# Layer 1's feed forward by seven products of halves, in program order

## The chip, the core and the metric

The kernel runs on one core of one Trainium2 chip. The metric is the time of one execution in microseconds of device time. A core has five engines that run side by side, each taking its own instructions in order: PE (TensorE, matrix products), DVE (VectorE), ACT (ScalarE), POOL (GpSimd) and SP, which issues the DMA transfers here.

## The reference

Two layers of a transformer block over 512 latent and 256 context tokens of width 1024. Cut to what the change touches:

```python
def swiglu(h, w1, w3, w2):
    return (jax.nn.silu(h @ w1) * (h @ w3)) @ w2
...
    x = x + gt1 * merge_branches(...)
    x = x + gt2 * swiglu(modulate(rms_norm(x, norm2[l]), sh2, sc2), w_ff1[l], w_ff3[l], w_ff2[l])
```

Layer 0 does this for all 768 tokens, layer 1 (the last) for the 512 latent tokens only. The hidden width is 2816, which is 22 blocks of 128.

## The kernel before

Everything is fp32, and each product is made from split operands: a tile x is cut into a rounded part `hi` and the rest `lo = x - hi`, and a product of 128x128 weights with activations is three matmuls (w_hi a_hi, w_hi a_lo, w_lo a_hi). `split` (L293) issues the cast of `hi` on ACT (L294) and the subtraction of `lo` on DVE or POOL (L295). Activations lie with channels on the partitions and tokens along the free axis, so a matmul's width is the number of tokens it takes.

Weights come in pieces of 128x512 floats (256 KB) into a ring of five `ws` tiles, and their `hi` and `lo` go into rings of four (`wh`, `wl`).

**Layer 0's feed forward** takes blocks in pairs. `ff_pair` makes the two blocks of a pair for the two halves of the tokens (384 each) by seven products instead of eight, in the manner of Strassen and Winograd: once for w1 with silu, once for w3 with the multiplication. Each of the two calls `pair_product` (L423), whose seven products need four sums of weight pieces (s1, s2, s4, s3, on DVE, L341), seven casts on ACT, six `lo` subtractions on DVE and one on POOL. In `pair_product`, a PSUM bank A takes products 1, 3, 5 and 7, a bank B products 2 and 4, a bank C product 6; between them ACT copies what A or B holds at that point (L444, L447, L449, L453), and the next product adds on to the same bank. The activations' sums, which the pairs share, are made once by `pair_forms` from the norm's output. `flow` (L317) prepares each piece three products ahead. This part stands under `tc.manual_schedule()`, so the engines execute it in the order in which it is written; elsewhere a scheduler sets the order. The first pair (blocks 0 and 1) is done by `first_pair` with plain products of halves, during which `pair_forms` runs. The output products (w2) take the results four blocks at a time, in the parts (0,4), (4,8) and so on.

**Layer 1's feed forward** is written differently: `plain` makes each block with 24 matmuls for w1 and 24 for w3, 512 tokens wide (block 0 in two halves of 256 while the norm still runs), then `keep_u` splits the result, and `ff2_j` makes the output products of the blocks 0 to 7, 8 to 14 and 15 to 21. The scheduler sets the order of it all. Before it, `lagged(wo_j, ...)` makes the attention output products and the norm, half by half.

Of the kernel before, what the change touches and what calls it, by code (L numbers as in the profile page):

```python
# [16 lines left out]
P = 128  # L17
# [13 lines left out]
CS = (SEQ, NT)  # L31
HT = NT // 2
NG = 2
WM0 = 4
# [6 lines left out]
def dit_block(ctx: ExitStack, tc: tile.TileContext, xT, ctxn, conds, vecs, ident_in, rope_c, rope_s,  # L41
# [69 lines left out]

    arena, homes = {}, ["AB"]

    def new_arena(*which):
        for i in which:
            tag = homes[0][i // 8]
            arena[i] = big.tile([P, 4 * HT], F32R, tag=tag, name=tag, bufs=8)

    def unit(i, n=HT):
        return arena[i // 4][:, i % 4 * HT:i % 4 * HT + n]  # L120

    def pair_at(i, n=HT):
        step = 1 if n <= HT else 2
        return unit(i, n), unit(i + step, n)
# [157 lines left out]
    def cut_piece(st, n, kinds="hl"):  # L282
        lo_rot[0] += 1
        eng = lo_engs[0][lo_rot[0] % len(lo_engs[0])]
        if kinds == "bb":
            t = big.tile([P, 4 * HT], F32R, tag=homes[0][1], name="wb", bufs=8)
# [105 lines left out]
    def half_of(k, t):  # L392
        return pair_at(8 * (k % 4) + 4 * t + 2 * (k // 4))

    def sum_of(i, kk):
        return pair_at(32 + 8 * kk + 4 * (i % 2) + 2 * (i // 2))

    def split_two(t, u, eng):

        d = arena[u // 4].rearrange("p (v h n) -> p h v n", h=2, n=HT)  # L400
        split(t, d[:, 0], d[:, 1], eng)

    def pair_forms(Y, kk):

        y = Y[kk].rearrange("p (b n) -> p b n", n=HT)
        new_arena(8 + 2 * kk, 9 + 2 * kk)

        def two_forms():
            t = big.tile([P, 2 * HT], F32, tag="tf", name="tf", bufs=2)
            return t.rearrange("p (b n) -> p b n", n=HT)  # L410
        ta = two_forms()
        nc.vector.tensor_tensor(ta, y[:, 0:4:3], y[:, 1:2].to_broadcast([P, 2, HT]), op=ALU.subtract)
        tb = two_forms()
        nc.vector.tensor_tensor(tb[:, 0], y[:, 3], ta[:, 0], op=ALU.add)
        split_two(ta, 32 + 8 * kk, nc.vector)
        nc.vector.tensor_tensor(tb[:, 1], y[:, 2], tb[:, 0], op=ALU.subtract)
        split_two(tb, 36 + 8 * kk, nc.vector)

    def four(name):

        return [area(name) for i in range(4)]

    def pair_product(take, tmp, ev11, ev12, ev21, ev22, extra):  # L423
# [14 lines left out]
        def bank():  # L438
            return next_bank()[:, :HT]

# [82 lines left out]
    def norm_half(X, G, S, t, Y):  # L523

        a, b = t * HT, (t + 1) * HT
        RB = norm_stats(X, a, b)
        yield
        if t == 0:
            for kk in range(4):
                Y[kk] = big.tile([P, 4 * HT], F32, tag="Y", name="Y", bufs=PAIRS["Y"])  # L530
        for kk in range(4):
            y4 = Y[kk].rearrange("p (b n) -> p b n", n=HT)
# [62 lines left out]
    for l in range(2):  # L595
# [641 lines left out]
        gate_src = Z[7][0]  # L1237
        h2 = new_h(W) if last else new_halves()
        Y2 = {}
# [15 lines left out]

        if last:
            lagged(wo_j, segs, halves, lambda p: norm(Xn, G2[l], MOD[l][:, 3], *p, h2))
        else:
            lagged(wo_j, segs, [(0, HT), (HT, NT)], lambda p: norm_half(Xn, G2[l], MOD[l][:, 3], p[0] // HT, Y2))
        X = Xn  # L1260


        def plain(f0, f1, U):
            for n in range(f0, f1):
                first = n == 0
                sg = halves if first else segs
                su = area("su", W)

                def ev1(D, a, b):
                    nc.scalar.activation(su[:, a:b], D, AF.Silu)  # L1270

                def ev3(D, a, b):
                    nc.vector.tensor_tensor(su[:, a:b], su[:, a:b], D, op=ALU.mult)
# [18 lines left out]
        def first_pair(U):  # L1292

            su = [area("su") for _ in range(2)]
            ks = (0, 4, 1, 5, 2, 6, 3, 7)
            ww = {}

            def go(n, i, t):
                o = su[n][:, t * HT:(t + 1) * HT]
                turn[0] += 1  # L1300
                D = wide[turn[0] % 2][:, turn[0] // 2 % 2 * 512:][:, :HT]
                mm([D], [ww[n, i][k] for k in ks], [half_of(k, t) for k in ks], [(0, HT)])
                if i == 0:
# [14 lines left out]
        def ff_pair(m, U, take):  # L1318
            sa, sb = area("su"), area("su")
            a1, a2, b1, b2 = sa[:, :HT], sa[:, HT:], sb[:, :HT], sb[:, HT:]  # L1320

# [33 lines left out]

        def ff_layer_0(parts):

            items = []
            for f0, f1 in parts:
                items += [(True, w_13[l, i, 2 * m:2 * m + 2]) for m in range(f0 // 2, f1 // 2) if m for i in range(2)]  # L1360
                if f1 < NFF:
                    items += [(False, w_2[l, j][:, f0:f1, :].rearrange("p k n -> p (k n)")) for j in range(KD)]
            U = []
            first_pair(U)
            with tc.manual_schedule():
                for _ in range(3):
                    load_1()
                take = flow(items)
                for pi, (f0, f1) in enumerate(parts):
                    if pi:  # L1370
                        U, spot[0] = [], 0
                    for m in range(f0 // 2, f1 // 2):
                        if m:
                            ff_pair(m, U, take)
                    if f1 == NFF:
# [3 lines left out]
                    w, D = {}, {}  # L1379

                    def some(j, ks):
                        if j not in w:
                            wh, wl = take(j == 1)
                            w[j] = [(wh[:, i:i + P], wl[:, i:i + P]) for i in range(0, 512, P)]
                            D[j] = [next_bank() for _ in segs]
                        for k in ks:
                            mm(D[j], w[j][k:k + 1], U, segs, k=k)

                    for j in range(KD):
                        if j == 0:  # L1390
                            some(0, (0, 1))
                            some(1, (0, 1))
                            some(0, (2, 3))
                        else:
                            some(j, range(4) if j > 1 else (2, 3))
                        if j >= 2 or pi > 1:
                            sums_layer_1()
                        for d, (a, b) in zip(D[j], segs):
                            c = int(a >= SEQ)
                            nc.vector.scalar_tensor_tensor(X[j][:, a:b], d[:, :b - a], MOD[l][:, 5, j, c:c + 1],  # L1400
                                                           X[j][:, a:b], op0=ALU.mult, op1=ALU.add)

        parts = [(0, 8), (8, 15), (15, 22)] if last else [(0, 4), (4, 8), (8, 12), (12, 16), (16, 22)]
        if not last:
            U = ff_layer_0(parts)
            new_wide()
            parts = parts[-1:]
        for pi, (f0, f1) in enumerate(parts):
            if last:
                U = []  # L1410
                plain(f0, f1, U)
            if f1 == NFF and not last:
                homes[0] = "BA"
                hnext = new_h()
            def ff2_j(j, sg):
                w = load_w(w_2[l, j][:, f0:f1, :], f1 - f0)

# [4 lines left out]
                gemm(w, U, sg, ev)  # L1422
                if f1 == NFF:
                    a, b = sg[0][0], sg[-1][1]
                    if last:
                        nc.sync.dma_start(out[j], X[j][:, :SEQ])
                    else:
                        nc.sync.dma_start(xspill[j][:, a:b], X[j][:, a:b])

            if f1 == NFF and not last:  # L1430
                lagged(ff2_j, segs, halves, lambda p: norm(X, G1[1], MOD[1][:, 0], *p, hnext), KD)
            else:
                for j in range(KD):
                    ff2_j(j, segs)

# [64 lines left out]
```

## Time and profile before

| | us |
|---|---|
| median of 3 runs | 1927.59 (1927.42 to 1928.4) |
| the profiled execution's own time | 1930.93 |
| its span, from the first to the last instruction | 1929.1 |
| PE busy in that span | 1866.0 (97%) |
| DVE, ACT and POOL busy | 1143.4, 823.4, 702.4 |
| from layer 1's first feed forward matmul to the end of the span | 1561.57 to 1929.1 |

Matmuls overlap, so a row's duration of one matmul is longer than the distance to the next; the distance is read from the chain of waits or the timeline, as the length of a piece over its count. In a timeline row stand the start, the duration, the engine, the line, the operation, the tiles, and in brackets the idle time before it and what ended that.

### The profile page before, as it was taken

The numbers are of one execution on the slowest core, as the hardware profiler recorded it, in microseconds if no ns is written. First come the engines' busy times: TensorE is split into PE (matmuls) and PEld (weight loads), VectorE is DVE, ScalarE is ACT, GpSimd is POOL, SyncE is SP. The second block draws the span as 40 slices with busy tenths as digits, with TensorE's granted clock in tenths as the row PEclk, the third lists the DMA queues.
The fourth block names the chain that finished last, engine by engine and source line by source line (L and its number), as shares of the span: only waits on it lengthen the run. The fifth ranks groups of instructions, "written<-read, shape, count | busy, mean of one in ns | idle before, by whom it ended". The sixth has DMA issues, their size and how long they took to land.

```text
span 1929.1 us, 27661 instructions
## 1 busy us (share of the span) xinstructions
PE 1866.0 (97%) x10146; PEld 1647.7 (85%) x10146; DVE 1143.4 (59%) x1866; ACT 823.4 (43%) x1544; POOL 702.4 (36%) x572
## 2 busy tenths in 40 slices
PE   5998999999999899999999999999999999999999
PEld 4778989888889899998989988878788888888887
DVE  7678886586456978876767675267633461222222
ACT  3546866422224534342525455456533353233232
POOL 4543543442223322122222457653332343333231
PEclk9999999999999999999999999999999999999999
DMA  8653210343354143435342263321033443333333
GB/s 301 219 204 102 70 50 29 120 159 121 105 212 136 46 133 111 152 108 164 116 159 98 80 210 102 105 64 33 19 108 99 142 124 96 98 99 89 103 95 96
DMA packets 109449, 225.58 MB, mean 117 GB/s; under 512 B 12288, under 2 KB 21248, under 8 KB 109184
## 3 DMA queue, kind: packets, MB, share of 16 engines
q1 hardware_dynamic: 108208, 221.96, 35.8%
q10 hardware_dynamic: 1104, 1.84, 0.3%
q8 instruction: 80, 1.31, 0.3%
q14 instruction: 57, 0.47, 0.1%
HBM read 215.89 MB, written 5.24 MB: 115 GB/s over the span
## 4 chain that ended last, share of the span: by engine, by line
PE 55%; DVE 3%; ACT 1%; issue 1%; POOL 1%; DMA 0%; ACTq 0%; DVEq 0%; POOLq 0%
PE pD L304 17%; PE wide L304 16%; PE pE L435 12%; PE pE L304 5%; PE pF L304 2%; PE pO L1157 1%; PE pPT L1150 1%; PE wide L1124 1%; DVE nm L1128 1%; POOL u L295 0%; DVE ny L495 0%; DVE pt L1154 0%; ACT work L1131 0%; DVE B L500 0%; DVE nacc L471 0%
## 5 line engine op out<-in xcount | busy, mean ns | idle before, releaser
L295 POOL TENSOR_TENSOR wl<-ws,wh 128x512 fp32r<-128x512 f32 (+2 forms) x274 | 364.4, 1333 | 745.5 <-ACT wh L294 704.1
L294 ACT CAST wh<-ws 128x512 fp32r<-128x512 f32 (+2 forms) x534 | 322.2, 608 | 675.8 <-PE pD L304 219.1
L295 DVE TENSOR_TENSOR wl<-ws,wh 128x512 fp32r<-128x512 f32 x260 | 199.8, 770 | 311.9 <-ACT wh L294 309.5
L304 PE MATMUL wide<-B,wh 128*128 128x512 f32 (+1 forms) x816 | 230.6, 372 | 4.5 <-DVE B L500 1.9
L304 PE MATMUL pD<-B,wh 128*128 128x512 f32 (+1 forms) x720 | 218.4, 384 | 0.1
L304 PE MATMUL wide<-A,wh 128*128 128x512 f32 (+2 forms) x608 | 162.2, 360 | 13.4 <-POOL A L295 6.6
L304 PEld LDWEIGHTS wide<-B,wh 128*128 128x128 f32 x816 | 144.9, 189 | 33.1 <-DVE B L500 2.5
L435 PE MATMUL pE<-B,wh 128*128 128x384 f32 x640 | 162.6, 334 | 1.1 <-ACT work L444 1.0
L304 PEld LDWEIGHTS pD<-B,wh 128*128 128x128 f32 x720 | 134.1, 189 | 26.4 <-POOL B L295 0.3
L304 PE MATMUL wide<-B,wl 128*128 128x512 f32 (+1 forms) x408 | 143.8, 373 | 0.1
L304 PE MATMUL pD<-B,wl 128*128 128x512 f32 (+1 forms) x360 | 138.0, 384 | 0.0
L181 DVE SCALAR_TENSOR_TENSOR work<-work,fixed 128x1024 f32<-128x1024 f32 x80 | 112.7, 1408 | 37.2 <-DMA work<-in_w_modT 35.4
L304 PEld LDWEIGHTS wide<-A,wh 128*128 128x128 f32 x608 | 105.6, 191 | 33.4 <-POOL A L295 8.7
L304 PE MATMUL pD<-A,wh 128*128 128x512 f32 (+1 forms) x544 | 130.6, 349 | 0.1
L435 PE MATMUL pE<-A,wh 128*128 128x384 f32 x480 | 121.8, 334 | 0.0
L435 PEld LDWEIGHTS pE<-B,wh 128*128 128x128 f32 x640 | 115.5, 188 | 1.9 <-ACT work L444 1.8
L435 PE MATMUL pE<-B,wl 128*128 128x384 f32 x320 | 106.9, 334 | 0.0
L304 PEld LDWEIGHTS pD<-A,wh 128*128 128x128 f32 x544 | 88.4, 189 | 14.8 <-ACT wh L294 0.4
L304 PE MATMUL wide<-A,wl 128*128 128x512 f32 (+2 forms) x304 | 99.9, 358 | 0.3 <-DVE wl L295 0.3
L1133 POOL TENSOR_SCALAR work<-work,nm 128x768 f32<-128x768 f32 x64 | 59.9, 936 | 87.8 <-DVE nm L1132 70.2
L295 DVE TENSOR_TENSOR wl<-work,wh 128x512 fp32r<-128x512 f32 x80 | 80.7, 1014 | 15.8 <-ACT wh L294 15.7
L435 PEld LDWEIGHTS pE<-A,wh 128*128 128x128 f32 x480 | 86.5, 188 | 0.2
(308 smaller groups left out, 3947.2 us busy)
## 6 DMA issues: line engine op xcount, KB each, us to landing
ws<-in_w SPq DMA_DIRECT2D x256, 256.0 KB, 2.7
work<-in_w_modT SPq DMA_DIRECT2D x112, 512.0 KB, 4.4
ws<-in_w_in SPq DMA_DIRECT2D x184, 256.0 KB, 2.6
ws<-in_w_o SPq DMA_DIRECT2D x48, 256.0 KB, 2.6
ws<-in_w_abc SPq DMA_DIRECT2D x32, 256.0 KB, 2.6
ws<-in_w_six SPq DMA_DIRECT2D x16, 192.0 KB, 5.2
xr<-in_xT SPq DMA_DIRECT2D x8, 384.0 KB, 8.0
ws<-in_w SPq DMA_DIRECT2D x16, 192.0 KB, 2.3
```

The costliest lines, as they stand in the source:

```text
L181: nc.vector.scalar_tensor_tensor(o, t, 1.0, sbc[:, c, :], op0=ALU.mult, op1=ALU.mult, accum_out=MOD[l][:, sec, b, c:c + 1])
L294: nc.scalar.copy(hi, src)
L295: (lo_eng or nc.gpsimd).tensor_tensor(lo, src, f(hi), op=ALU.subtract)
L304: nc.tensor.matmul(d[:, :b - a], lhsT=ww, rhs=aa[:, a:b], start=kk == 0 and i == 0, stop=kk == n - 1 and i == 2)
L435: nc.tensor.matmul(D, lhsT=x[:, kk * P:(kk + 1) * P], rhs=a, start=not more and kk == 0 and i == 0, stop=kk == 3 and i == 2, skip_group_ch ...
L1124: nc.tensor.matmul(D[:, a - k0:b - k0], lhsT=q[:, c * P - q0:(c + 1) * P - q0], rhs=kt[:, a:b], start=i == 0, stop=i == 1)
L1128: nc.vector.tensor_reduce(nm[:, 0:1], D[:, :nk], axis=AX.X, op=ALU.max, negate=True)
L1133: nc.gpsimd.tensor_scalar(pt[:, :nk], pt[:, :nk], nm[:, 3:4], 0.0, op0=ALU.mult, op1=ALU.add)
L1150: nc.tensor.transpose(TD[:, (2 * j + cc) * P:(2 * j + cc + 1) * P], pts[cc][:, kc:kc + P], ident)
L1157: nc.tensor.matmul(o[:, 0:256], lhsT=v3[:, kt, :], rhs=pp[:, j * 256:(j + 1) * 256], start=gi == 0 and j == 0 and i == 0, stop=gi == len(k ...
```

## The change

Layer 1's feed forward takes the path of layer 0: `first_pair`, ten `ff_pair`s and output products in program order, now in the function `ff` for both layers. A half is `hw[0]` tokens wide: 384 in layer 0, 256 in layer 1. The norm of layer 1 becomes `norm_half`, which writes Y for `pair_forms`. Layer 1's parts become (0,8), (8,16), (16,22); an output product's weights come in pieces of four blocks. `plain` goes.

```diff
-        h2 = new_h(W) if last else new_halves()
+        hw[0] = W // 2
+        new_halves()
...
-        if last:
-            lagged(wo_j, segs, halves, lambda p: norm(Xn, G2[l], MOD[l][:, 3], *p, h2))
-        else:
-            lagged(wo_j, segs, [(0, HT), (HT, NT)], lambda p: norm_half(Xn, G2[l], MOD[l][:, 3], p[0] // HT, Y2))
+        lagged(wo_j, segs, [(0, hw[0]), (hw[0], W)],
+               lambda p: norm_half(Xn, G2[l], MOD[l][:, 3], p[0] // hw[0], Y2))
...
-        def plain(f0, f1, U):
-            for n in range(f0, f1):
...
-                w1 = load_w(w_13[l, 0, n], KD)
-                gemm(w1, h2, sg, ev1, "D", first)
-                w3 = load_w(w_13[l, 1, n], KD)
-                gemm(w3, h2, sg, ev3, "D", first)
-                keep_u(su, U)
...
-        def ff_layer_0(parts):
+        def ff(parts):
...
-                            some(0, (0, 1))
-                            some(1, (0, 1))
-                            some(0, (2, 3))
+                            some(0, range(nk - 2))
+                            if nk <= 4:
+                                some(1, range(nk - 2))
+                            some(0, range(nk - 2, nk))
...
-        parts = [(0, 8), (8, 15), (15, 22)] if last else [(0, 4), (4, 8), (8, 12), (12, 16), (16, 22)]
-        if not last:
-            U = ff_layer_0(parts)
...
+        if last:
+            ff([(0, 8), (8, 16), (16, 22)])
+        else:
+            U = ff([(0, 4), (4, 8), (8, 12), (12, 16), (16, 22)])
```

**Three places in the order of instructions.** On every engine the order up to the middle of layer 1's second norm is the one before. The rows below are the program's own order; no time is in them.

DVE in the middle of layer 1's feed forward, before: two `lo` subtractions and one multiplication with PSUM (L1273), per block.

```order
L295 TENSOR_TENSOR wl<-ws,wh 128x512 x2
L1273 TENSOR_TENSOR work<-work,wide_9549 128x512
L295 TENSOR_TENSOR wl<-ws,wh 128x512 x2
L1273 TENSOR_TENSOR work<-work,wide_9549 128x512
L295 TENSOR_TENSOR wl<-ws,wh 128x512 x2
L1273 TENSOR_TENSOR work<-work,wide_9550 128x512
```

DVE now, from the fourth product of a pair's second half (w3) on: L1322, L1326, L1330 and L1335 take the products out, L342 makes the sums s1', s2', s4', s3' of the next pair's weights, L296 the `lo` of s1', s2', and last of s4' and s3'.

```order
L1322 TENSOR_TENSOR work<-work,pE 128x256
L342 TENSOR_TENSOR work<-ws 128x512
L1326 TENSOR_TENSOR work<-work 128x256
L342 TENSOR_TENSOR work<-work,ws 128x512
L296 TENSOR_TENSOR wl<-work,wh 128x512
L1330 TENSOR_TENSOR work<-work,pE 128x256
L342 TENSOR_TENSOR work<-work,ws 128x512
L296 TENSOR_TENSOR wl<-work,wh 128x512
L1335 TENSOR_TENSOR work<-work,pE 128x256
L342 TENSOR_TENSOR work<-ws 128x512
L296 TENSOR_TENSOR wl<-work,wh 128x512 x2
L296 TENSOR_TENSOR wl<-ws,wh 128x512 x2
```

The sums and the products' exits are new on DVE, and the weights' `lo` stand behind them.

ACT at the same place, before: casts of weights, one silu per block (L1270), one cast of a result (`u`).

```order
L294 CAST wh<-ws 128x512 x2
L1270 ACTIVATE work<-pD 128x512
L294 CAST wh<-ws 128x512 x2
L294 CAST u<-work 128x512
L294 CAST wh<-ws 128x512 x2
```

ACT now: the copy of product 5 (L455), the casts of s1', s2' and s4', the casts of the pair's two results `u`, and only then the copy of the next pair's first product (L446), which its third product waits for.

```order
L455 COPY work<-pE 128x256
L295 CAST wh<-work 128x512 x3
L295 CAST u<-work 128x512 x2
L446 COPY work<-pE 128x256
L295 CAST wh<-work 128x512
L449 COPY work<-pE 128x256
```

A copy that PE waits for now stands behind two casts that wait for the pair's last multiplications.

ACT at the entry, in the norm of the first half, before: the `hi` of the first chunk is one activation (L499), and the others follow one by one.

```order
L499 ACTIVATE B<-ny,fixed 128x256
L294 CAST wh<-ws 128x512
L502 ACTIVATE ny<-ny,fixed 128x256 x2
L294 CAST B<-ny 128x256
L499 ACTIVATE B<-ny,fixed 128x256
```

ACT there now: six activations (L541) and four casts of weights stand ahead of the first `hi` (`B_13057`, chunks 0 and 4).

```order
L541 ACTIVATE Y<-Y,fixed 128x256
L295 CAST wb<-ws 128x512
L295 CAST wh<-ws 128x512
L541 ACTIVATE Y<-Y,fixed 128x256 x2
L295 CAST wb<-ws 128x512
L541 ACTIVATE Y<-Y,fixed 128x256
L295 CAST wh<-ws 128x512
L541 ACTIVATE Y<-Y,fixed 128x256 x2
L295 CAST B_13057<-Y 128x2x256
```

The first product's first operand has moved from the first place behind the norm's start to the eleventh.

More of the change, by code (lines that the diff above doesn't have):

```diff
@@ L419, in four @@
     def four(name):
-        return [area(name) for i in range(4)]
+        return [area(name, hw[0]) for i in range(4)]
     def pair_product(take, tmp, ev11, ev12, ev21, ev22, extra):
@@ L1292, in first_pair @@
         def first_pair(U):
-            su = [area("su") for _ in range(2)]
+            su = [area("su", W) for _ in range(2)]
             ks = (0, 4, 1, 5, 2, 6, 3, 7)
@@ L1360, in ff_layer_0 @@
                 items += [(True, w_13[l, i, 2 * m:2 * m + 2]) for m in range(f0 // 2, f1 // 2) if m for i in range(2)]
-                if f1 < NFF:
-                    items += [(False, w_2[l, j][:, f0:f1, :].rearrange("p k n -> p (k n)")) for j in range(KD)]
+                if last or f1 < NFF:
+                    items += [(False, w_2[l, j][:, k0:min(k0 + 4, f1), :].rearrange("p k n -> p (k n)"))
+                              for j in range(KD) for k0 in range(f0, f1, 4)]
             U = []
@@ L1365, in ff_layer_0 @@
             with tc.manual_schedule():
-                for _ in range(3):
-                    load_1()
+                if not last:
+                    for _ in range(3):
+                        load_1()
                 take = flow(items)
@@ L1374, in ff_layer_0 @@
                             ff_pair(m, U, take)
-                    if f1 == NFF:
+                    if f1 == NFF and not last:
                         while waiting:
@@ L1378, in ff_layer_0 @@
                         return U
-                    w, D = {}, {}
+                    w, D, nk = {}, {}, f1 - f0
                     def some(j, ks):
                         if j not in w:
-                            wh, wl = take(j == 1)
-                            w[j] = [(wh[:, i:i + P], wl[:, i:i + P]) for i in range(0, 512, P)]
-                            D[j] = [next_bank() for _ in segs]
+                            w[j], D[j] = [], [next_bank() for _ in segs]
                         for k in ks:
+                            if k == len(w[j]):
+                                wh, wl = take(j == 1 and k == 0)
+                                w[j] += [(wh[:, i:i + P], wl[:, i:i + P]) for i in range(0, min(nk - k, 4) * P, P)]
                             mm(D[j], w[j][k:k + 1], U, segs, k=k)
@@ L1401, in ff_layer_0 @@
                                                            X[j][:, a:b], op0=ALU.mult, op1=ALU.add)
-        parts = [(0, 8), (8, 15), (15, 22)] if last else [(0, 4), (4, 8), (8, 12), (12, 16), (16, 22)]
-        if not last:
-            U = ff_layer_0(parts)
-            new_wide()
[L1407 to L1414, printed above, removed]
+                        if f1 == NFF:
+                            nc.sync.dma_start(out[j], X[j][:, :SEQ])
+        if last:
+            ff([(0, 8), (8, 16), (16, 22)])
+        else:
+            U = ff([(0, 4), (4, 8), (8, 12), (12, 16), (16, 22)])
+            new_wide()
+            homes[0] = "BA"
+            hnext = new_h()
+            hw[0] = HL
             def ff2_j(j, sg):
-                w = load_w(w_2[l, j][:, f0:f1, :], f1 - f0)
+                w = load_w(w_2[l, j][:, 16:NFF, :], NFF - 16)
                 def ev(D, a, b):
@@ L1422, in ff2_j @@
                 gemm(w, U, sg, ev)
[L1423 to L1434, printed above, removed]
+                a, b = sg[0][0], sg[-1][1]
+                nc.sync.dma_start(xspill[j][:, a:b], X[j][:, a:b])
+            lagged(ff2_j, segs, halves, lambda p: norm(X, G1[1], MOD[1][:, 0], *p, hnext), KD)
 _OUT = (8, 128, 512)
```

58 lines of the change are left out of this document (27 added, 31 removed).

## The prediction

> **What bounds the kernel now.** I read the page's busy times first, then the chain of waits, then the stretches by engine.
>
> ```profile
> span 1929.1 us, 27661 instructions
> PE 1866.0 (97%) x10146; PEld 1647.7 (85%) x10146; DVE 1143.4 (59%) x1866; ACT 823.4 (43%) x1544; POOL 702.4 (36%) x572
> ...
> 822.60:880.70 58.10, 58.10 (x337) 58.10 (x336) 42.88 (x61) 28.13 (x52) 17.31 (x11) 1.00 0.37 118
> 1599.00:1777.20 178.20, 178.20 (x788) 147.56 (x787) 37.70 (x54) 54.89 (x91) 58.77 (x46) 1.00 0.32 96
> ```
>
> In a stretch's row stand its length, then the busy time of PE, weight loads, DVE, ACT and POOL, the granted clock, the DMA share and GB/s. PE never rests in layer 1's feed forward (1599 to 1777) nor in two pairs of layer 0 (822 to 881), at clock 1.00. So time there falls with PE's work, as long as nobody makes PE wait. DVE is where the two differ: 37.70 of 178.20 us against 42.88 of 58.10.
>
> What a matmul costs by its width comes from the chain:
>
> ```profile
> 1543.80 2.88 PE pD L304 x24
> ...
> 1604.51 5.44 PE wide L304 x24
> ```
>
> These are 256 and 512 tokens wide: 2.88/24 = 0.120 us, 5.44/24 = 0.227; layer 0's 384 take 58.10/337 = 0.172 in the stretch above. The 256-wide ones load new weights for each matmul, as the changed ones will.
>
> **The change part by part: PE.** A pair of blocks cost 2 x 48 matmuls at 0.227, 21.76 us; now 2 x 7 x 12 = 168 at 0.120, 20.16. Ten pairs: -16.0 us. This is less than an eighth, since narrow matmuls cost 6% more per token (0.120 against 0.113). The output products stay 8 x 22 x 3 = 528 matmuls of 512: 0. The end (last product's exit and its transfer) stays: 0.
>
> **The change part by part: the new waits.** A product now lasts 12 x 0.120 = 1.44 us, against 12 x 0.172 = 2.08 (rounded up) in layer 0, and DVE, ACT and POOL have to do much the same work per product. Whether they keep up is seen where a pair ends, in layer 0. DVE, from the fourth product of a w3 half:
>
> ```profile
> 1030.90 0.56 DVE L1337 TENSOR_TENSOR work<-work,pE 128x384 f32<-128x384 f32 x1 [0.36 <-PE pE L435]
> 1031.37 0.68 DVE L341 TENSOR_TENSOR work<-ws 128x512 f32<-128x512 f32 x1
> 1033.49 1.11 DVE L1341 TENSOR_TENSOR work<-work 128x384 f32<-128x384 f32 x1 [1.44 <-ACT work L453]
> 1034.52 0.68 DVE L341 TENSOR_TENSOR work<-work,ws 128x512 f32<-128x512 f32 x1
> 1035.12 1.50 DVE L295 TENSOR_TENSOR wl<-work,wh 128x512 fp32r<-128x512 f32 x1
> 1036.55 0.54 DVE L1345 TENSOR_TENSOR work<-work,pE 128x384 f32<-128x384 f32 x1
> 1037.01 0.68 DVE L341 TENSOR_TENSOR work<-work,ws 128x512 f32<-128x512 f32 x1
> 1037.62 1.50 DVE L295 TENSOR_TENSOR wl<-work,wh 128x512 fp32r<-128x512 f32 x1
> 1039.04 0.54 DVE L1350 TENSOR_TENSOR work<-work,pE 128x384 f32<-128x384 f32 x1
> 1039.50 0.68 DVE L341 TENSOR_TENSOR work<-ws 128x512 f32<-128x512 f32 x1
> 1040.11 4.58 DVE L295 TENSOR_TENSOR wl<-work,wh 128x512 fp32r<-128x512 f32 x2
> ```
>
> POOL and ACT at the same time:
>
> ```profile
> 1031.60 1.34 POOL L1338 TENSOR_TENSOR work<-work 128x384 f32<-128x384 f32 x1 [12.95 <-DVE work L1337]
> 1032.89 1.29 POOL L295 TENSOR_TENSOR wl<-ws,wh 128x512 fp32r<-128x512 f32 x1
> 1034.74 1.33 POOL L1342 TENSOR_TENSOR work<-work 128x384 f32<-128x384 f32 x1 [0.56 <-DVE work L1341]
> 1037.17 1.40 POOL L1346 TENSOR_TENSOR work<-work 128x384 f32<-128x384 f32 x1 [1.09 <-DVE work L1345]
> 1039.51 4.62 POOL L295 TENSOR_TENSOR A<-work,A 128x768 fp32r<-128x768 f32 x2 [0.94 <-ACT A L294]
> ...
> 1032.98 0.48 ACT L453 COPY work<-pE 128x384 f32<-128x384 f32 x1 [1.63 <-PE pE L435]
> 1038.60 0.84 ACT L294 CAST A<-work 128x768 fp32r<-128x768 f32 x1 [0.18 <-POOL work L1346]
> 1039.61 0.84 ACT L294 CAST A<-work 128x768 fp32r<-128x768 f32 x1 [0.17 <-DVE work L1350]
> 1040.35 0.47 ACT L444 COPY work<-pE 128x384 f32<-128x384 f32 x1
> ```
>
> Read DVE's `lo` of 0.69 us at rest: it takes 1.50 where POOL works (1035.12: POOL's L1342 ends at 1036.07, the `lo` 0.55 later), and 2.3 each where POOL splits the results. POOL's turn comes as late: 1.34 for what scales to about 1.0. DVE and POOL shut each other out, in turns, when DVE reads two SBUF tiles; DVE's reads of PSUM (0.54 to 0.56) are not touched. So the path is a chain through both: exit of product 4, a multiplication and a split on POOL, exit of product 5, sum, POOL, `lo`, exit of 6, sum, POOL, `lo`, exit of 7, cast of the second result, copy L444. From product 4's end (about 0.26 before 1030.90, as 1032.98 stands to product 5's) it ends at 1040.82: 10.2 us. Product 3 of the next pair adds on to that bank and starts five products after product 4's end: 5 x 2.08 = 10.4. Layer 0 has 0.2 us to spare. One pair earlier (1.22 us of a modulation sum in DVE's queue shortly before) it has none, and PE waits:
>
> ```profile
> 751.13 1.22 DVE L243 SCALAR_TENSOR_TENSOR work<-work,fixed 128x1024 f32<-128x1024 f32 x1
> ...
> 762.84 0.84 ACT L294 CAST A<-work 128x768 fp32r<-128x768 f32 x1 [0.17 <-DVE work L1350]
> 763.58 0.48 ACT L444 COPY work<-pE 128x384 f32<-128x384 f32 x1
> ...
> PE pE L435 <- ACT work L444: 1.0, 1, 1.0
> ```
>
> In layer 1 the window is 5 x 1.44 = 7.2 us. The chain's weight sums and `lo`s are still 512 wide; only what is as wide as the tokens shrinks. Durations at 256 and 512 tokens:
>
> ```profile
> 1580.43 0.42 DVE L1273 TENSOR_TENSOR work<-work,wide 128x256 f32<-128x256 f32 x1 [0.17 <-ACT work L1270]
> 1580.02 0.38 ACT L1270 ACTIVATE work<-wide 128x256 f32<-128x256 f32 x1
> 1567.16 0.74 POOL L295 TENSOR_TENSOR B<-ny,B 128x256 fp32r<-128x256 f32 x1
> 1582.69 1.30 POOL L295 TENSOR_TENSOR u<-work,u 128x512 fp32r<-128x512 f32 x1
> 1580.94 0.62 ACT L294 CAST u<-work 128x512 fp32r<-128x512 f32 x1
> ```
>
> Four DVE exits save 0.14 each (0.42 for 0.56), three POOL multiplications 0.28 each (half of 1.30 - 0.74, for 128 fewer of 256), the cast 0.22 (0.62 for 0.84) and the copy 0.1: about 1.7 in all. The chain is 10.2 - 1.7 = 8.5 us in a window of 7.2: PE waits 1.3 us before product 3. Behind it come the `lo`s of s4' and s3', between POOL's two splits of 1.30. If DVE's sum s3' gets in first, s4' is ready in time and s3' is 0.1 late; if POOL does, s4' is 1.0 later. So 1.3 to 2.3 us per transition; the rows at 1039.50 and 1039.51 show a dead heat, so I take the middle, 1.8. Within the parts there are 2 + 3 + 2 = 7 such transitions: +12.6. From zero, if POOL's turns fall into DVE's idle time after all, to 16.1.
>
> The pieces themselves arrive just in time:
>
> ```profile
> DMA to landing us min/median/max: 2.5/2.9/4.6
> ```
>
> That is the feed forward of layer 0. The ring's tiles come free with the sum s3', 8.1 to 9.2 us into the chain, so the next pieces land at 11.0 to 12.5, and the next half's first sum, behind product 4's exit, stands at about 12: 0, at most 0.5 per transition, within the range of the wait.
>
> From w1's half to w3's of the same pair POOL has only one split of 1.29; the same chain there gives about 6.4 us against 7.2: 0.8 to spare, no wait. Where a pair is followed by output products (three times), no sums stand in between; the second result is ready about 4.4 us after product 7, and PE has 18 matmuls of 0.227 (4.1 us) to do first, in the last part 12 (2.7 us): +0.7 (0 to 1.5).
>
> **The entry.** Products of the first pair: before 96 x 0.120 + 48 x 0.227 = 22.4, now 192 x 0.120 = 23.0: +0.6.
>
> ```profile
> 1559.25 1.64 DVE L495 SCALAR_TENSOR_TENSOR ny<-xr,fixed,pRB 128x256 f32<-128x256 f32 x4
> 1559.75 0.51 ACT L499 ACTIVATE B<-ny,fixed 128x256 fp32r<-128x256 f32 x1
> 1561.57 0.52 PE L304 MATMUL pD<-B,wh 128*128 128x256 f32 x3
> ...
> 1925.08 0.39 PE L304 MATMUL wide<-u,wl 128*128 128x512 f32 x1
> ```
>
> From 1561.57 to 1925.31 PE needs 96 x 0.120 + 1536 x 0.2267 = 359.7 of 363.7 us, so 4.0 go to the norm's own matmuls and waits. Now the first `hi` stands behind six activations and four casts, each 0.1 less than its row's 0.51 or 0.62 where they follow each other: 1559.75 + 4.5 + 0.6 = 1564.8, a first wait of 3.3. Later products wait less, for a third product of the first half (2.9 us) is done while the second half's norm runs; but POOL's `lo` of each chunk pair and about 28 us of DVE work (27 instructions of 512 elements at 0.60, 16 of the norm at 1.64/4 = 0.41, 15 smaller at 0.34) lie in 23 us of PE. I take 6 us of waits and norm for 4: in all +2.5, from -1 (the later products hide everything) to +6 (DVE's 28 us plus a few POOL turns).
>
> Sum: -16.0 + 12.6 + 0.7 + 2.5 = -0.2 us on a span of 1929.1. The profiled execution (1930.93) lies 3.3 us over the median; I apply the difference to the median: 1927.4.
>
> [...] The trace shows DVE's `lo` held until POOL's instruction ends. [...] Its chance, 0.12, is a part of the forecast's 0.42, whose own range holds it. [...]
>
> **Rivals.** PE stays the bound (0.28): the dead heat falls well, and the POOL multiplications slip into DVE's 1.44 us of idle time before the exit of product 5, so that the chain shortens below 7.2. For: PE idles nowhere in 58 us of layer 0 shown above. Against: 1.3 us too long by rows. Then -16.0 + 0.7 + 2.5 = -12.8: 1914.8; half the waits gives 1921.
>
> The wait doesn't heal (0.30), ending slower: after the transition DVE is 1 us behind, the w1 half's chain has 0.8 to spare, and past that point its third product waits too, ten times by about 1.0, with 2.3 at each of the seven. For: the stall at 763 came from just such extra DVE work. Against: between products 2 and 4 DVE has little to do. -16.0 + 16.1 + 10.0 + 0.7 + 2.5 = +13.3: 1940.9.
>
> **How the numbers follow.** Forecast 0.42, its own range 1921 to 1934 (waits of 9 to 16 us, entry -1 to +6). About 0.2% (3.9 us) is what a measurement of this kernel can tell from no change. Of the forecast's 0.42, most lies within; the edges are balanced by the near sides of the rivals: faster 0.30, same 0.39, slower 0.31. The range takes in the faster rival's centre and nearly the slower one's: 1914 to 1940.
>
> **What would show it.** Right: 256-wide pE matmuls 0.120 apart; seven PE waits of 1.3 to 2.3 us for L446's copy or for DVE's `lo` (L296), each one product or two into a pair; DVE's `lo`s of 1.3 to 2 us beside POOL; PE's busy share falling in that stretch while DVE's passes 75%. Wrong: a pair of 20.2 us without waits, waits in the w1 half, or DVE and ACT waiting for pieces from DMA by more than half a microsecond.

## The result, and the profile after

| | before | after |
|---|---|---|
| median, us | 1927.51 (1925.94 to 1928.4, 4 runs) | 1938.68 (1938.06 to 1939.85, 4 runs) |
| ratio, with its 95% interval | | 1.006 (1.0042 to 1.0077) |
| span of the profiled execution | 1929.1 | 1936.9 |
| last attention output product's end to the end of the span | 367.5 | 377.7 |

The changed kernel is slower by 11.2 us. The forecast was 1927.4: the sign of the sum was wrong, though the value lies within the range of 1914 to 1940.

The last row of the table, called the stretch below, is used to compare the kernels. Up to the middle of layer 1's second norm the instructions are the same ones in the same order (E3 apart), and yet the point where the stretch starts lay between 1557 and 1562 us in the profiles of this study. The stretch leaves that difference out, which a median holds. But each stretch is read from one profile, so small differences between two of them show little by themselves. In the kernel before it starts at 1561.57, where the first matmul of the feed forward follows the last output matmul without a gap; in the changed kernel at 1559.16, which is the last such matmul's start (1559.04) and 0.12. So the change cost 377.7 - 367.5 = 10.2 us there.

The page's totals and two stretches of the changed kernel (length; busy time of PE, weight loads, DVE, ACT, POOL; granted clock; DMA share; GB/s):

```profile
span 1936.9 us, 29624 instructions
PE 1858.9 (96%) x10914; PEld 1675.6 (87%) x10914; DVE 1314.4 (68%) x2117; ACT 889.5 (46%) x1703; POOL 691.2 (36%) x554
...
1559.16:1594.04 34.88, 27.92 (x201) 26.74 (x199) 27.28 (x45) 19.44 (x43) 15.30 (x10) 0.90 0.16 53
1701.00:1790.00 89.00, 84.58 (x675) 82.21 (x674) 72.53 (x106) 51.12 (x106) 30.80 (x24) 1.00 0.30 94
```

PE has 7 us less to do than before (1858.9 against 1866.0) and the kernel is longer all the same. In the four pairs of the second part (the last row) PE rests 4.4 of 89 us, where it never rested before, and DVE works 81% of the time. In the entry (the row above) PE is busy 27.9 of 34.9 us, and the granted clock is 0.90.

What PE waited for, from 1540 us on (us in total, times, longest):

```profile
PE pE L437 <- ACT work L446: 9.6, 8, 1.3
PE wide L305 <- ACT B L295: 3.6, 1, 3.6
PE wide L305 <- POOL B L296: 1.8, 1, 1.8
PE wide L305 <- ACT work L1289: 1.5, 2, 0.8
PE pE L437 <- DVE wl L296: 1.3, 6, 0.2
```

The first row and the last are the transitions from pair to pair; the three between are the entry. One transition, by engine:

```profile
1634.55 0.73 POOL L1323 TENSOR_TENSOR work<-work 128x256 f32<-128x256 f32 x1 [8.38 <-DVE work L1322]
1634.80 1.03 DVE L342 TENSOR_TENSOR work<-ws 128x512 f32<-128x512 f32 x1 [0.40 <-DMA ws<-in_w]
1635.24 1.74 POOL L296 TENSOR_TENSOR wl<-ws,wh 128x512 fp32r<-128x512 f32 x1
1635.75 1.51 DVE L1326 TENSOR_TENSOR work<-work 128x256 f32<-128x256 f32 x1
...
1641.35 1.75 DVE L342 TENSOR_TENSOR work<-ws 128x512 f32<-128x512 f32 x1
1641.27 2.97 POOL L296 TENSOR_TENSOR u<-work,u 128x512 fp32r<-128x512 f32 x2 [0.73 <-ACT u L295]
1643.01 2.38 DVE L296 TENSOR_TENSOR wl<-work,wh 128x512 fp32r<-128x512 f32 x2
...
1641.46 0.62 ACT L295 CAST u<-work 128x512 fp32r<-128x512 f32 x1 [0.26 <-DVE work L1335]
1641.98 0.36 ACT L446 COPY work<-pE 128x256 f32<-128x256 f32 x1
...
1642.40 0.51 PE L437 MATMUL pE<-A,wh 128*128 128x256 f32 x2 [1.34 <-ACT work L446]
```

It is the chain that the prediction read from layer 0, in which DVE and POOL take turns. Where one of DVE's instructions that take two SBUF tiles starts while POOL works, it ends only after POOL's, in all 53 cases from 1594 to 1930 us; the six with a PSUM operand that start so take 0.41 to 0.42 us, as they do alone. The sum at 1634.80 takes 1.03 us beside a multiplication, and the exit at 1635.75 waits out POOL's split (1.51 us, 0.43 alone). At 1641.27 and 1641.35 POOL's split of the result and DVE's sum s3' start in a dead heat, and here POOL wins: the sum takes 1.75 us, not 0.68. ACT's copy L446 stands behind the cast of the second result and comes 1.3 us late.

The entry of the changed kernel, by engine:

```profile
1562.91 0.50 PE L305 MATMUL wide<-B,wh 128*128 128x256 f32 x2 [3.58 <-ACT B L295]
1565.22 0.58 PE L305 MATMUL wide<-B,wh 128*128 128x256 f32 x1 [1.81 <-POOL B L296]
...
1565.81 0.63 PE L305 MATMUL wide<-B,wh 128*128 128x256 f32 x2
...
1566.45 0.63 PE L305 MATMUL wide<-B,wh 128*128 128x256 f32 x2
...
1562.25 0.60 ACT L295 CAST B<-Y 128x512 fp32r<-128x512 f32 x1
...
1562.68 1.27 POOL L296 TENSOR_TENSOR wl<-ws,wh 128x512 fp32r<-128x512 f32 x1
1563.90 2.95 POOL L296 TENSOR_TENSOR B<-Y,B 128x512 fp32r<-128x512 f32 x2
```

PE waits 3.58 us for the first `hi`, does two matmuls and waits 1.81 us for its `lo`, because POOL is still at a `lo` of weights. And then this, the same stretch of the clock in both kernels, the changed one's row first:

```profile
1564.25:1571.05 6.80, 5.83 (x28) 5.83 (x28) 4.87 (x5) 1.27 (x3) 2.60 (x2) 0.50 0.33 116
...
1564.00:1571.00 7.00, 5.39 (x41) 4.80 (x40) 5.57 (x13) 3.96 (x11) 3.89 (x5) 1.00 0.14 47
```

Behind the two waits the granted clock is 0.50 for 6.8 us. PE counts as busy there, but its 256-wide matmuls stand 0.213 us apart instead of 0.120 (three from 1565.81 to 1566.45, above).

### The profile page after: what moved, and what is told of

Its sections match the earlier page's. It is cut to its first block, busy times and chain, and to the rows that moved or that the text cites. A ratio compares the mean times of both kernels' runs of the same rounds, so it can differ in the third digit from the quotient of the medians.

```text
span 1936.9 us, 29624 instructions
## 1 busy us (share of the span) xinstructions
PE 1858.9 (96%) x10914; PEld 1675.6 (87%) x10914; DVE 1314.4 (68%) x2117; ACT 889.5 (46%) x1703; POOL 691.2 (36%) x554
## 5 line engine op out<-in xcount | busy, mean ns | idle before, releaser
L296 POOL TENSOR_TENSOR wl<-ws,wh 128x512 fp32r<-128x512 f32 (+2 forms) x229 | 316.1, 1384 | 636.0 <-ACT wh L295 612.0
L296 DVE TENSOR_TENSOR wl<-ws,wh 128x512 fp32r<-128x512 f32 x283 | 215.5, 765 | 162.2 <-ACT wh L295 159.0
L437 PE MATMUL pE<-B,wh 128*128 128x384 f32 (+1 forms) x1120 | 252.6, 313 | 1.6 <-ACT work L446 1.0
L437 PE MATMUL pE<-A,wh 128*128 128x256 f32 (+1 forms) x1120 | 240.7, 306 | 9.6 <-ACT work L446 9.6
L437 PEld LDWEIGHTS pE<-A,wh 128*128 128x128 f32 x1120 | 186.2, 190 | 11.4 <-ACT work L446 11.2
L437 PE MATMUL pE<-B,wl 128*128 128x384 f32 (+1 forms) x560 | 175.8, 314 | 1.3 <-DVE wl L296 1.3
L437 PE MATMUL pE<-A,wl 128*128 128x256 f32 (+1 forms) x560 | 170.7, 305 | 0.0
L305 PE MATMUL pE<-u,wh 128*128 128x512 f32 x608 | 164.1, 367 | 0.9 <-POOL u L296 0.9
L296 DVE TENSOR_TENSOR wl<-work,wh 128x512 fp32r<-128x512 f32 x160 | 151.9, 956 | 18.3 <-ACT wh L295 16.9
L305 PEld LDWEIGHTS pE<-u,wh 128*128 128x128 f32 x608 | 105.1, 188 | 20.6 <-POOL u L296 2.0
L437 PEld LDWEIGHTS pE<-B,wl 128*128 128x128 f32 x560 | 106.1, 189 | 2.9 <-DVE wl L296 2.7
L305 PE MATMUL pD<-B,wh 128*128 128x512 f32 (+1 forms) x352 | 108.5, 388 | 0.0
L437 PEld LDWEIGHTS pE<-A,wl 128*128 128x128 f32 x560 | 106.5, 190 | 0.0
```

Of the source, the lines that this page charges most:

```text
L296: (lo_eng or nc.gpsimd).tensor_tensor(lo, src, f(hi), op=ALU.subtract)
L305: nc.tensor.matmul(d[:, :b - a], lhsT=ww, rhs=aa[:, a:b], start=kk == 0 and i == 0, stop=kk == n - 1 and i == 2)
L437: nc.tensor.matmul(D, lhsT=x[:, kk * P:(kk + 1) * P], rhs=a, start=not more and kk == 0 and i == 0, stop=kk == 3 and i == 2, skip_group_ch ...
```

## The experiments

All edits are to the changed kernel. In the table, "stretch" is the time from the last attention output product's end to the end of the span in the profiled execution, and "half clock" is how long the granted clock was 0.50 at the entry, summed from rows of half a microsecond. E4, E9, E10 and E11 contain 28 extra matmuls whose results nobody uses; nothing is left out of any of them.

| kernel | stretch | half clock | median, us | ratio to before, 95% interval |
|---|---|---|---|---|
| before | 367.5 | 0 | 1927.51 | |
| after | 377.7 | 6.82 | 1938.68 | 1.006 (1.0042 to 1.0077) |
| E1 | 370.4 | 6.83 | 1931.11 | 1.0018 (1.0009 to 1.0028) |
| E2 | 377.4 | 6.83 | 1939.62 | 1.0062 (1.0047 to 1.0077) |
| E3 | 376.0 | 6.82 | 1939.04 | 1.0061 (1.0046 to 1.0076) |
| E4 | 375.1 | 0 | 1936.41 | 1.0046 (1.0029 to 1.0063) |
| E5 | 365.8 | 6.83 | 1926.33 | 0.9991 (0.9981 to 1.0) |
| E6 | 364.7 | 6.82 | 1924.31 | 0.9981 (0.9972 to 0.999) |
| E7 | 364.3 | 6.83 | 1925.23 | 0.9984 (0.9974 to 0.9993) |
| E8 | 375.4 | 3.41 | 1937.10 | 1.0045 (1.003 to 1.006) |
| E9 | 362.0 | 0 | 1923.84 | 0.9977 (0.9966 to 0.9987) |
| E10 | 362.2 | 0 | 1924.67 | 0.9984 (0.9975 to 0.9993) |
| E11 | 377.9 | 6.83 | 1938.23 | 1.0052 (1.0039 to 1.0064) |

E1 to E4 ran beside the kernel before at a median of 1927.77, E5 to E8 at 1928.21, and E9 to E11 at 1928.87.

### E1: the multiplications of the w3 half on DVE

```diff
+        mul_eng = nc.vector if last else nc.gpsimd
...
-                nc.gpsimd.tensor_tensor(a2, a2, x, op=ALU.mult)
+                mul_eng.tensor_tensor(a2, a2, x, op=ALU.mult)
```

The same is done for b2 and a1.

> The changed kernel (1938.7 us), but in layer 1 the three multiplications of a pair's w3 half run on DVE, behind the exits that feed them, and no longer on POOL. Theory (the chain of turns between DVE and POOL makes the second result late, and with it ACT's cast of it and the copy L446 that PE waits for): a POOL turn of about 0.65 us plus hand-over becomes 0.34 us on DVE, three times, the chain shortens by about 1.2 us, PE's waits for L446 fall from 9.6 us to under 2, those for DVE's lo stay about 1: 1927 to 1930 us. Rival (ACT has too much to do there, two casts of results and two of weights between two copies): ACT's work is the same, the waits for L446 stay near 9.6: 1937 to 1940.

The stretch fell by 7.3 us, and PE's waits for DVE's `lo` are gone. The median, 1931.11, lies 1.1 us above its range, for L446 is still waited for.

```profile
PE pE L437 <- ACT work L446: 7.9, 8, 1.0
...
1610.73 0.43 DVE L1325 TENSOR_TENSOR work<-work 128x256 f32<-128x256 f32 x1
1611.08 1.78 DVE L342 TENSOR_TENSOR work<-ws 128x512 f32<-128x512 f32 x1
...
1610.77 1.54 POOL L296 TENSOR_TENSOR wl<-ws,wh 128x512 fp32r<-128x512 f32 x1 [8.79 <-ACT wh L295]
```

A multiplication on DVE takes 0.43 us and no turn is given away. But POOL's one remaining split at the head of the chain, that of the piece a11, now meets the sum s1' (1.78 us for 0.68): the chain starts 1.1 us late and stays so. E1 alone doesn't tell the turns from POOL's slower multiplication (0.73 us in the changed kernel); E5 does.

### E2: the second result's split one product later

```diff
-                behind(1, lambda: keep_u(sb, U))
+                behind(1 + late, lambda: keep_u(sb, U))
```

Here `late` is 1 where another pair follows in the same part.

> The changed kernel, but within a part the second result of a pair is cast and split one product later, so that ACT's copy L446 no longer stands behind that cast. Theory (the whole chain is late, DVE's sum s3' too): the wait for L446 falls to about 0.4 each, but the copy of the second product (L449) then stands behind the cast of s3' and of the result and makes PE wait about 0.5: of 1.87 us per transition some 0.9 to 1.3 are left, 1932 to 1935 us. Rival (the order on ACT alone is the matter): the waits go, and nothing takes their place: 1927 to 1930.

No gain, and the median is above both ranges. ACT's copy L446 no longer stands behind the second cast, and its waits fall from 9.6 to 3.5 us; but the next copy, L449, behind which the cast has moved, takes them over:

```profile
PE pE L437 <- ACT work L449: 10.1, 7, 1.5
...
PE pE L437 <- ACT work L446: 3.5, 8, 1.0
...
1640.64 1.76 DVE L342 TENSOR_TENSOR work<-ws 128x512 f32<-128x512 f32 x1
...
1640.57 1.29 POOL L296 TENSOR_TENSOR u<-work,u 128x512 fp32r<-128x512 f32 x1 [0.73 <-ACT u L295]
```

POOL starts the first result's split 0.07 us ahead of the sum s3', and the sum is as late as before. So ACT's order alone is not the cause. It is mostly the place where the lateness of DVE and POOL is seen.

### E3: the last six attention output products by halves, in place of four

```diff
-               lambda p: norm_half(Xn, G2[l], MOD[l][:, 3], p[0] // hw[0], Y2))
+               lambda p: norm_half(Xn, G2[l], MOD[l][:, 3], p[0] // hw[0], Y2), 6 if last else 4)
```

This gives the first half's norm more time ahead of the feed forward.

> The changed kernel, but in layer 1 the last six attention output products are made half by half, not the last four, so that two more products of 2.88 us stand between the first half's end and its feed forward (cost: 0.64 us for the narrower matmuls, four more pieces loaded and cast). Theory (the first half's norm is late, PE waits 3.6 and 1.8 us for it, and its clock then falls to 0.60 for 7 us): all three go, -7 + 0.6: 1931 to 1934 us, and the granted clock at the entry stays 1.00. Rival (DVE's and ACT's work at the entry as a whole is the limit, 28 us of DVE): the waits move to the second half's products and to the first pair's start, at most -2: 1936 to 1939.

The first wait of 3.6 us is gone, and one of 3.54 stands in the second half instead. The order that results there puts sums of the next pair's weights, which wait for a transfer, ahead of the norm on DVE:

```profile
1572.49 0.69 DVE L342 TENSOR_TENSOR work<-ws 128x512 f32<-128x512 f32 x1 [3.52 <-DMA ws<-in_w]
...
1574.03 3.21 DVE L539 SCALAR_TENSOR_TENSOR Y<-xr,fixed,pRB 128x256 f32<-128x256 f32 x8
...
1576.67 0.79 PE L305 MATMUL wide<-B,wh 128*128 128x256 f32 x2 [3.54 <-ACT B L295]
```

The wait moved, and the 6.8 us of half clock moved with it. The median, 1939.04, lies just above the rival's range and far from the theory's.

### E4: extra matmuls in the gap of the entry

```diff
+            if last:
+                fill = pst("O")
+                for _ in range(28):
+                    nc.tensor.matmul(fill[:, :256], lhsT=Z[7][0][:, 0:P], rhs=Z[7][0][:, 256:512], start=True, stop=True)
             first_pair(U)
```

> The changed kernel with 28 extra matmuls of 256 in layer 1, on finished operands into a bank that nobody reads; 24 of them stand right ahead of the feed forward's first matmul, where PE idles 3.6 us. Theory (24 matmuls of the first product ran 0.213 apart, since the idle time had lowered the granted clock to 0.60): the clock stays at 1.00, these 24 run 0.120 apart: -2.2 us, 1936 to 1937. Rival (they are 0.213 apart because they wait for operands): no change, 1938 to 1940.

The stretch fell by 2.6 us and the median by 2.3, as expected. The first product starts no earlier (4.2 us behind the output products, against 3.75 in the changed kernel), but the clock stays at 1.00:

```profile
1562.00:1570.00 8.00, 5.54 (x44) 5.33 (x45) 4.53 (x6) 3.74 (x9) 5.00 (x5) 1.00 0.38 131
```

The expectation's 0.60 is the mean from 1562.90 to 1570.30; the clock itself was 0.50 in part of that and 1.00 in the rest. So the half clock alone costs 2.3 to 2.6 us: some 28 matmuls (the row of 1564.25 above) by 0.213 - 0.120 is 2.6.

### E5 and E6: no split of weights on POOL, and then the second result later

E5 is E1 with the `lo` of a11 on DVE in layer 1 too; E6 is E5 with the edit of E2.

```diff
-            todo += [(lambda i=a11: raw[i], nc.gpsimd), (total("s1", a21, a22, ALU.add), nc.vector),
+            todo += [(lambda i=a11: raw[i], a11_eng), (total("s1", a21, a22, ALU.add), nc.vector),
...
-                take = flow(items)
+                take = flow(items, 3, mul_eng)
```

> As the kernel with the multiplications on DVE (1931.1 us), and in layer 1 also the one weight split per half that POOL had (piece a11) on DVE; POOL keeps the splits of the results alone. Theory (the chain that ends in ACT's cast of the second result and the copy L446 is too long for 7.2 us; in that run DVE's sum s1' took 1.78 us beside POOL's split of a11): the chain loses about 0.9 us more, PE's waits for L446 fall from 0.99 to 0.1 to 0.3 each: 1924 to 1926 us. Rival (ACT's order and load set the wait): it stays at 0.8 to 1.0: 1930 to 1932.

> As e5, and within a part the second result is cast and split one product later. Theory: with the chain short enough, the copies L446 and L449 both find ACT free, no wait over 0.2 us is left at the seven transitions: 1923 to 1925 us. Rival (late casts only push the wait to the next copy, as in the run with the late cast alone): 1925 to 1928.

E5 came out 0.3 us above its range, E6 within it. The first row below is E5's, the others are E6's:

```profile
PE pE L437 <- ACT work L446: 4.1, 8, 0.8
...
PE pE L437 <- ACT work L446: 0.6, 2, 0.4
...
1743.19 0.68 DVE L342 TENSOR_TENSOR work<-ws 128x512 f32<-128x512 f32 x1
1743.49 0.37 ACT L446 COPY work<-pE 128x256 f32<-128x256 f32 x1
1743.67 1.35 POOL L296 TENSOR_TENSOR u<-work,u 128x512 fp32r<-128x512 f32 x1 [17.64 <-ACT u L295]
...
1701.00:1790.00 89.00, 89.00 (x701) 86.68 (x700) 76.73 (x130) 53.34 (x110) 11.61 (x8) 1.00 0.34 110
```

POOL now has only the split of the results, and in E6 it comes 0.5 us behind the sum s3'. PE is busy throughout the second part's pairs, although DVE is busy for longer than in the changed kernel (76.73 us against 72.53). By the distances of the matmuls, the seven transitions cost 15.8 us in the changed kernel, 8.7 in E1, 5.7 in E5 and 3.9 in E6, where one of them still waits 0.4 us for L446. E5 moves a split that the chain does not need, leaves ACT's order as it is and gives DVE more to do. So most of the time was lost because DVE and POOL took turns, and not because DVE had too much work; what ACT's order adds is the 1.8 us between E5 and E6.

E6 takes 13.1 us off the stretch and is faster than the kernel before, by 3.9 us in the median. The edit of E2, which was worth nothing alone, takes 1.1 us off the stretch once the chain is on time.

### E7 and E8: every `lo` of the norm on DVE

E7 is E6 with this edit, E8 the changed kernel with this edit alone.

```diff
-            split_two(y4[:, t:4:2], 8 * kk + 4 * t, nc.vector if kk % 2 else nc.gpsimd)
+            split_two(y4[:, t:4:2], 8 * kk + 4 * t, nc.vector if kk % 2 or hw[0] == HL else nc.gpsimd)
```

> As e6, and in layer 1's norm all lo of the activations on DVE (before, every second on POOL). Theory (at the entry PE waited 1.8 us for POOL's first lo, with 1.3 us of its own and behind two splits of weights, while DVE idled 2.2 us): that wait falls to about 0.3, the granted clock comes up sooner: 2 to 3 us below e6: 1920 to 1923. Rival (28 us of DVE work at the entry is the limit, so more of it on DVE costs): no gain or slower than e6.

> The changed kernel with that one edit of the norm alone (all lo of the activations on DVE in layer 1). Theory: the second wait at the entry (1.8 us) falls to about 0.3, the time by 2 to 3 us: 1936 to 1937. Rival (DVE is the limit at the entry): 1938 to 1940.

E8's median came out at the upper end of its range, E7's above it: E7's stretch is only 0.4 us shorter than E6's. The entry shows why one edit seemed worth 2.3 us of the stretch in E8 and nothing in E7. In both, the wait for POOL's `lo` is replaced by two for DVE's (this row reads alike in both):

```profile
PE wide L305 <- DVE B L296: 1.6, 2, 1.0
```

And E8's clock was at half for one piece of 3.41 us, E7's for two (6.83). In E8 PE was busy all through that piece; in E7 it was busy 2.65 us of the first one (1565.94 to 1569.35). The rows, E8's only:

```profile
1564.25:1567.50 3.25, 3.25 (x16) 3.25 (x17) 1.95 (x4) 0.99 (x3) 0.00 (x0) 0.50 0.67 242
1567.50:1570.90 3.40, 3.40 (x30) 3.40 (x30) 1.84 (x4) 0.34 (x1) 0.70 (x1) 0.99 0.00 0
```

That piece is worth about 16 matmuls by 0.093 = 1.5 us, most of E8's gain. The edit itself gives little: 0.4 us of E7's stretch.

### E9, E10 and E11: the entry's edits on E6, and alone

E9 is E6 with E4's extra matmuls. E10 is E9 with the edit of E7 and four of the first half's eight biases on DVE. E11 is the changed kernel with the entry's three edits.

```diff
+                    if n == HL and t == 0 and kk > 1:
+                        nc.vector.tensor_scalar(y[:, u - a:v - a], y[:, u - a:v - a], S[:, k, c:c + 1], None, op0=ALU.add)
+                        continue
                     nc.scalar.activation(y[:, u - a:v - a], y[:, u - a:v - a], AF.Identity, bias=S[:, k, c:c + 1])
```

> E6 with E4's 28 extra matmuls of 256 behind the attention output products (their results are not used). The extra matmuls took 2.3 us off the changed kernel, and E6's entry has the same wait of 3.8 us and the same granted clock of 0.59 behind it. Theory (the entry's clock and the seven transitions are separate costs, which add): 1924.3 - 2.3 = 1922.0, 1921 to 1923. Rival (without the waits at the transitions PE runs from the entry on behind DVE, so a faster first pair is given back in the next ones, as in E7): 1924 to 1925.

> E9, with E7's edit (every lo of the norm on DVE) and the bias of chunks 2, 3, 6 and 7 of the first half added on DVE in place of ACT, so that the first hi stands behind four activations instead of six (about 0.9 us of ACT). Theory (ACT's queue and POOL's first lo set the start of the first product): both early waits fall, 1922.0 - 0.9 - 0.7 = 1920.4, 1919.5 to 1921.5. Rival (the first pair ends when DVE has done with its 28 us, and each instruction moved to DVE makes the later waits longer): 1922 to 1924.

> The changed kernel with the three edits of the entry alone (extra matmuls, lo of the norm on DVE, four biases on DVE); the transitions stay. Theory (entry and transitions add): 1938.7 - 2.3 - 1.6 - 0.9 = 1933.9, 1933 to 1935, with the waits of 1.87 us at the seven transitions unchanged. Rival (DVE is the bound in the first pair): 1936 to 1937.

E9's stretch fell by 2.7 us, as the theory says. Its median lies above the 1921 to 1923 that were expected, on a chip where the kernel before was slower too; the intervals of E6 and E9 overlap, so the gain is read from one trace and not shown by the times. E9 has the lowest median of the study, 0.9977 (0.9966 to 0.9987) of the kernel before.

E10 and E11 missed, and lie above their rivals' ranges too. The biases on DVE make the exit of the last attention output product late, and its PSUM bank is needed (L1259 is the changed kernel's L1256, that exit; the first two rows are E10's, the other two E11's):

```profile
1566.80 0.38 PE L305 MATMUL wide<-B,wh 128*128 128x256 f32 x1 [2.05 <-DVE xr L1259]
1566.70:1573.50 6.80, 5.70 (x45) 5.51 (x46) 4.48 (x12) 1.47 (x4) 0.70 (x1) 1.00 0.48 154
...
1562.58 0.38 PE L305 MATMUL wide<-B,wh 128*128 128x256 f32 x1 [1.83 <-DVE xr L1259]
1563.30:1570.10 6.80, 6.13 (x29) 6.13 (x29) 4.14 (x8) 0.71 (x2) 0.00 (x0) 0.50 0.43 152
```

The two kernels have the same entry and nearly the same waits. In one the clock stayed, in the other it fell to 0.50, although the extra matmuls had run just ahead: PE did 45 matmuls in 6.8 us in one, and 29 in the other. So the extra matmuls did not always keep the clock; the last section sets the two side by side.

## Why the prediction was wrong, step by step

The total of 10.2 us in the stretch, against the prediction's terms:

| term | predicted | measured |
|---|---|---|
| PE's ten pairs | -16.0 | -16.0, by the matmuls' distance |
| seven transitions | +12.6 | +15.8 |
| the entry | +2.5 | +8.5 |
| ends of the parts, and behind the first pair | +0.7 | +1.9 |
| sum | -0.2 | +10.2 |

- **PE.** Right. The 256-wide matmuls stand 0.120 apart (1640.54 to 1640.78 for two), so ten pairs cost what the sum says.
- **The transitions.** Right in mechanism, and within the bounds in size: 2.2 to 2.4 us each, where 1.8 was taken between 1.3 and 2.3. A transition has a gap of 1.38 us at the copy L446 (1.50 in one of the seven), up to 0.5 behind late `lo`s, and some gaps of 0.1 us in the matmuls behind. Read from the distances of the matmuls from 1594 us on, all seven come to 15.8, just below the 16.1 of the upper bound. The dead heat went to POOL. E1, E5 and E6 show that the turns between DVE and POOL made most of the waits; E2, that ACT's order alone did not. The case to which the prediction gave 0.12, that all of DVE's and POOL's instructions of a pair stand in one line, no run shows: in the changed kernel's row of 1701, DVE's 72.53 and POOL's 30.80 us, 103.3 together, lie within 89.
- **The entry.** This is the step that failed: its term was mis-sized, 8.5 us where 2.5 was said and 6 was the upper end. It makes 6.0 of the 10.4 us by which the sum was off; the transitions make 3.2 and the last term 1.2. The place lasts 34.9 us (the row of 1559.16), 11.9 more than the 23.0 that its matmuls need; the prediction allowed 6. Of the 11.9, 6.9 are waits for operands, 2.6 the clock, and the rest the norm's own matmuls and small gaps. The first wait was foreseen (3.58 for 3.3). The second was named ("POOL's `lo` of each chunk pair") but not priced: 1.81 us, since POOL's queue was read without the `lo` of weights ahead. The two waits for silu (1.5 us) were not seen. And the clock was taken as 1.00 throughout, as in the rows of before: a wait of 3.3 us was predicted, but not what it does to the clock, which is 2.6 us more, shown by E4. The step "later products wait less" held for the waits (3.58, 1.81, then 0.69 and 0.84 us). But it treated the waits as the only cost, and here they slowed the matmuls behind them.
- **Behind the first pair and at the ends.** The first product pair after the first blocks waits for L446 as well (0.97 us by the profile; 1.4 us with the small gaps behind it), behind the split of the first blocks' results. This was not foreseen. The ends of the parts took 0.5 for 0.7.
- **What stays open.** Gaps of 0.1 us in the products behind a transition are there in E6 too, some 3.5 us in all, without a wait for L446 in most of them. The trace names nothing that PE waits for there.
- **DMA.** As bounded: the sum at 1634.80 waits 0.40 us for its piece, and the bound was 0.5.

Of the rivals, "the wait doesn't heal" gave 1940.9, close to the measured 1938.7, but for a reason that did not happen: no wait of PE stands between the w1 and the w3 half of a pair. The time alone would have credited it. "PE stays the bound" gave 1914.8; with the transitions mostly cured (E6) the kernel is 3.9 us faster instead of 12.8, because the entry keeps its 8 us where 2.5 was assumed, and the gaps of 0.1 us stay.

Of the entry, E4, E9 and E10 recover the clock's part. PE's waits for operands there, 6.9 us in the changed kernel, still come to 4 to 5 in E9 to E11, beside 2.9 us of extra matmuls that fill a part of them, whatever was moved among ACT, DVE and POOL. What a better order of the norm could give was not tried.

## What to carry to other kernels

When a step is made shorter for PE, lay the other engines' whole chain for that step beside the new window, with the turns that DVE and POOL take. A chain that just fitted can become the bound, as it did here, and the cure here was to take the second engine out of it, even though the first got more work. Where a change makes PE wait, price the matmuls behind the wait at half the clock too: behind the waits of 3.58 and 1.81 us here they stood 0.213 us apart instead of 0.120, for 6.8 us. Compare variants by the stretch that they alter as well as by the median, since here the rest of the program moved by up to 4 us, more than most edits were worth.

## What was not expected of the hardware

The granted clock falls to exactly 0.50 behind the waits of the entry, and stays there for 6.82 or 6.83 us in eight of the changed kernels (the changed kernel itself, E1, E2, E3, E5, E6, E7, E11), 3.41 us in E8 and not at all in E4, E9 and E10. These are two, one and no pieces of 3.41. The clock came back behind a piece in which PE was busy throughout: the first in E8, and the second in E7, where PE was busy for 2.65 us of the first. The falls lie whole pieces apart. By the traces' clock records the clock also falls once near 1152 us in most kernels (at 1151.29 in the changed kernel), and from there to the fall at the entry it is 409.60 us in E1, E5 and E6, 413.01 or 413.02 in the changed kernel, E7 and E11, and 423.26 in E3: 120, 121 and 124 pieces of 3.413.

The piece ahead of the fall was not always idle. Counting pieces of 3.413 back from the fall, PE was wholly idle in the last one in E2 only; by the profile it was busy for 0.39 to 0.52 us of it in the changed kernel, E1, E3 and E5 to E8, and for 1.18 us in E11. Where the clock did not fall, the emptiest piece of the entry, counted on from an earlier change of the clock, held 1.82 us of work in E4, 2.05 in E9 and 1.88 in E10. E11 (the first row) and E10 (the other two) beside each other:

```profile
1559.94:1563.35 3.41, 1.18 (x6) 0.58 (x4) 3.41 (x7) 1.68 (x4) 1.64 (x2) 1.00 0.05 7
...
1562.85:1566.26 3.41, 1.90 (x16) 1.70 (x14) 3.41 (x3) 1.98 (x5) 2.84 (x2) 1.00 0.00 0
1566.26:1569.68 3.42, 1.88 (x13) 1.69 (x14) 3.42 (x10) 1.45 (x3) 0.00 (x0) 1.00 0.66 189
```

In E11 nearly all of the waiting falls into one piece, and in E10 it is shared by two. So at this entry the clock fell behind a piece with 1.18 us of work or less in nine kernels, and stayed in the three whose emptiest piece held 1.82 or more. That the work in a piece is what decides was not shown, nor where a limit would lie. The pieces lay differently at the same entry, and no edit here set that, so whether an edit of the entry kept the clock may have been in part luck.
